# A transformer layer on one core: GpSimd's subtractions and gate products move to VectorE, and the attention output's loads become large tiles

## The chip, the cores and the metric

One core of one Trainium2 chip runs the whole layer as one program. The metric is device microseconds of one execution of that program. The engines are called PE (matrix products), DVE (VectorE), ACT (ScalarE), POOL (GpSimd) and SP (SyncE, which issues every DMA of this kernel, in order).

## What is computed

The reference, cut to the part around the change (1024 positions, 1024 features, all float32):

```python
h = h + 0.5 * swiglu(rms_norm(h, norm_ffn1), ffn1_gate, ffn1_up, ffn1_down)
u = rms_norm(h, norm_mix)
xc, bg, cg, q, k, v, g_conv, g_attn = split(u @ w_in)
y_conv = short_gated_conv(xc, bg, cg, conv_w) @ w_conv_out
q, k = apply_rope(q), apply_rope(k)              # 4 heads, two q/k sets of 64 each, v of 128
# for each block of 128 queries: p = softmax(mask(q k^T / 8)); a = p[set 0] - lam * p[set 1]
o = a @ v
o = rms_norm(o, subln_g) * (1 - lambda_init)     # per head, over its 128 features
y_attn = o @ w_attn_out
h = h + (sigmoid(g_conv) * y_conv + sigmoid(g_attn) * y_attn) @ w_o
h = h + 0.5 * swiglu(rms_norm(h, norm_ffn2), ffn2_gate, ffn2_up, ffn2_down)
return rms_norm(h, norm_final)
```

## The kernel before

Everything is kept feature-major (128 features on the partitions, 512 positions in a tile's row). A float32 product is made of three PE products of two halves: each operand is split into a rounded high part (`hi`, a copy) and what is left (`lo`, a subtraction), and hi·hi, hi·lo and lo·hi are summed in PSUM. So each operand that PE reads costs one copy, mostly on ACT (L248), and one subtraction of a 128x512 tile (L243), on DVE or on POOL: `split` (L245) has two fractions, and its share counter sends that part of the subtractions to POOL.

The program runs in stages, one after the other: the first feed-forward block (to about 640 us), the input projection of the mixer, **attention** (about 1013 to 1228 us), the **conv output**, the **heads' norm**, the **attention output**, the product with **w_o** (from 1334.5 us) and the second feed-forward block.

**Attention** (`attend`) goes over 16 units, a unit being a head and a pair of query blocks of 128. A unit has four scores (two query blocks, two sets); each is some matmuls (L955) with a mask product (L957), a row maximum on DVE (L966), an exponential on ACT (L972, L973), then a scaling on POOL (L981), the subtraction of the second set on DVE (L987 to L989), transposes on PE (L1001), their split, and the product with v (L1031). The k and q tiles are split by hand: high part on ACT (L943 for q), low part on POOL (L919 for k, 16 times, L944 for q, 16 times). Between these steps `fill()` puts pieces of six matmuls of other work on PE: first the gates of the mixer (`plain`, L1159), which is the remainder of the input projection, then blocks of the conv output. Within this part the order on PE, DVE, ACT and POOL is the order of the code (`manual_schedule`); after it a scheduler orders them. A unit uses two PSUM banks for scores ("sc"), two for transposes ("at"), one for its result ("ot"), and one ("ps") is left for the filling work.

**Conv output and attention output** are both `merge`: 16 blocks, a block being 12 matmuls of 128x512 (L1221) for 128 output features and half of the positions (t). For each block one gate tile (L1199) and, once per 128 features, one weight tile (L1192) are loaded into tiles of the pool C, which has ten. Conv blocks are evicted by an ACT copy (L1229) and a POOL multiply with the gate (L1230); attention blocks get a sigmoid on ACT (L1201), a DVE multiply (L1236) and a DVE add. The **heads' norm** (`normed`) lies between them: for each half t and head a square on ACT (L1293), a product with ones on PE (L1295), `rstd_light` (L446 to L450, three C tiles, its product on POOL) and a DVE multiply (L1300). Then `res` (L267 the matmuls, L398 the eviction) makes the product with w_o.

The piece that sets the order of the filling work before, and the eviction of a conv block:

```python
                if c == 6:
                    yield
...
                def ready(ms=ms, ps=ps, g=g):
                    nc.scalar.copy(ms, ps)
                    nc.gpsimd.tensor_tensor(ms, ms, g, ALU.mult)
```

`ready` runs at the next `settle()` of `attend`, that is right behind the next score.

Of the kernel before, what the change touches and what calls it, by code (L numbers as in the profile page):

```python
# [12 lines left out]
F32 = mybir.dt.float32  # L13
# [5 lines left out]
P = 128  # L19
# [140 lines left out]
class K:  # L160
# [281 lines left out]
    def rstd_light(self, ps, n):  # L442

        nc = self.nc
        y, v, a = self.C(), self.C(), self.C()
        nc.scalar.activation(y, ps, AF.Abs_reciprocal_sqrt, bias=self.eps, scale=1.0 / n)  # L446
        nc.vector.tensor_scalar(v, ps, 0.5 / n, 0.5 * EPS, ALU.mult, ALU.add)
        nc.scalar.activation(a, y, AF.Square)
        nc.gpsimd.tensor_tensor(v, a, v, ALU.mult)
        nc.vector.scalar_tensor_tensor(a, v, -1.5, y, ALU.add, ALU.mult)  # L450
        return a
# [309 lines left out]
class Mixer:  # L761
# [139 lines left out]
    def head(self, h):  # L901
# [6 lines left out]
        for s in range(2):  # L908
# [7 lines left out]
            for a, kd in enumerate(kds):  # L916
                ks = kst[:, s, a * TH : (a + 1) * TH]
                nc.scalar.copy(ks, kd)
                nc.gpsimd.tensor_tensor(ks[64:128], kd[64:128], ks[64:128].bitcast(F32), ALU.subtract)  # L919
# [14 lines left out]
    def load_q(self, h, qp):  # L934
# [9 lines left out]
        nc.gpsimd.tensor_tensor(qs[:, 1], qraw, qs[:, 0].bitcast(F32), ALU.subtract)  # L944
# [102 lines left out]
    def attend(self, fill, late):  # L1047
# [11 lines left out]
        for n in range(len(units) + 2):  # L1059
# [57 lines left out]
            if n >= 13:  # L1117
                next(late, None)
            last = p


    def plain(self, idxs, f):
# [3 lines left out]
        for x in ((0, 1),):  # L1126
# [3 lines left out]
            for c in range(4):  # L1130
                k.split(u[:, c], hi[:, c], lo[:, c], 0.7, 0.5, "pl")
# [4 lines left out]
        def weights(i, o):  # L1136
# [3 lines left out]
            for kk in range(2):  # L1140
                a = k.t("F", [P, 2, 4, P], F32R)
                k.split(raw[i][:, o, 4 * kk : 4 * kk + 4, :], a[:, 0], a[:, 1], 1.0, 0.5, "pw")
# [36 lines left out]
    def split_y(self, src):  # L1179
        k = self.k  # L1180
        r = k.t("Q", [P, 2, 2, TH], F32R)
        for j in range(2):
            k.split(src[:, j], r[:, 0, j], r[:, 1, j], 0.7, 0.4, "y")
        return r

    def merge(self, w, yq, wsrc, m):

        k, nc = self.k, self.k.nc

        def weights(n, j, o):  # L1190
            raw = k.t("C", [P, 4, P])
            nc.sync.dma_start(raw, wsrc[j][:, o])  # L1192
            a = k.t("FA"[n % 2] if w == 1 else "F", [P, 2, 4, P], F32R)
            k.split(raw, a[:, 0], a[:, 1], 1.0, 0.5 if w == 0 else 0.0, "ma")
            return a

        def gates(j, o, t):
            g = k.C()
            nc.sync.dma_start(g, self.gd[w][j][:, 2 * o + t, :])  # L1199
            if w == 1:  # L1200
                nc.scalar.activation(g, g, AF.Sigmoid, bias=self.gate_bias(w, j, o))  # L1201
            return g

        todo = [(j, o) for j in range(4) for o in range(2)]
        if w == 0:
            seq = [(x, t) for n in range(0, 8, 2) for t in range(2) for x in todo[n : n + 2]]
        else:
            seq = [(x, t) for t in (1, 0) for x in todo]
        ws = {x: weights(n, *x) for n, x in enumerate(todo[:2])}
        for n, ((j, o), t) in enumerate(seq):  # L1210
            g = gates(j, o, t)
            a = ws[j, o]
            self.settle()
            ps = k.psd() if self.dense else k.ps()
            c = 0
            for kk in range(4):
                if c == 6:
                    yield
                b = yq[kk // 2][t]
                for x, y in ((0, 0), (0, 1), (1, 0)):  # L1220
                    nc.tensor.matmul(ps, a[:, x, kk], b[:, y, kk % 2], start=c == 0, stop=c == 11)  # L1221
                    c += 1
            if len(ws) < 8 and (w == 1 or n % 4 > 1):
                ws[todo[len(ws)]] = weights(len(ws), *todo[len(ws)])
            ms = m[o][t][:, j]
            if w == 0:

                def ready(ms=ms, ps=ps, g=g):
                    nc.scalar.copy(ms, ps)  # L1229
                    nc.gpsimd.tensor_tensor(ms, ms, g, ALU.mult)  # L1230

                self.ready = ready
                if self.dense:
                    self.settle()
            else:
                nc.vector.tensor_tensor(g, ps, g, ALU.mult)  # L1236
                k.tt(ms, ms, g, ALU.add)
            yield
# [4 lines left out]
    def run(self, raws, f, load_h, done, pre):  # L1243
# [18 lines left out]
        with k.tc.manual_schedule(engines={ET.PE, ET.DVE, ET.Activation, ET.Pool}):  # L1262
# [3 lines left out]
            def values():  # L1266

                for t in range(2):
                    for a in range(2):
# [5 lines left out]
                        for j in range(2):  # L1275
                            k.split(y[j], yq[a][t][:, 0, j], yq[a][t][:, 1, j], 1.0, 1.0, "y")
# [3 lines left out]
            def normed():  # L1280

                Y = {}
                for t in (1, 0):
                    Y[t] = k.t("Q", [P, 4, TH])
                    for a in range(2):
                        nc.sync.dma_start(Y[t][:, 2 * a : 2 * a + 2], self.od[a][t])
                for t in (1, 0):
                    pss = []
                    for a in range(2):
                        oq[a][t] = k.t("Q", [P, 2, 2, TH], F32R)  # L1290
                    for i in range(4):
                        sq = k.C()
                        nc.scalar.activation(sq, Y[t][:, i], AF.Square)  # L1293
                        pss.append(k.psd())
                        nc.tensor.matmul(pss[i], k.ones, sq, start=True, stop=True)  # L1295
                        yield
                    for i in range(4):
                        y = Y[t][:, i]
                        r = k.rstd_light(pss[i], P)
                        nc.vector.scalar_tensor_tensor(y, y, self.gsub, r, ALU.mult, ALU.mult)  # L1300
# [155 lines left out]
```

## Time and profile before

| | |
|---|---|
| median of 3 runs | 2081.24 us (2080.03 to 2082.38) |
| the profiled execution | 2082.11 us |
| span of its profile | 2080.3 us |
| PE busy | 1981.0 us (95%) |
| DVE busy | 1402.0 us (67%) |
| ACT busy | 935.1 us (45%) |
| POOL busy | 136.8 us (7%) |
| mean granted PE clock | 0.978 of full speed |

A profile row names a line of the kernel, an engine, an operation and the tiles that it writes and reads; "[1.74 <-ACT Q L973]" behind a row says that the engine stood idle for 1.74 us before it, and which instruction's end released it. A granted clock of 1 is 2.4 GHz, 0.5 is 1.2 GHz.

### The profile page before, as it was taken

The numbers are of one execution on the slowest core, as the hardware profiler recorded it, in microseconds if no ns is written. First come the engines' busy times: TensorE is split into PE (matmuls) and PEld (weight loads), VectorE is DVE, ScalarE is ACT, GpSimd is POOL, SyncE is SP. The second block draws the span as 40 slices with busy tenths as digits, with TensorE's granted clock in tenths as the row PEclk, the third lists the DMA queues.
The fourth block names the chain that finished last, engine by engine and source line by source line (L and its number), as shares of the span: only waits on it lengthen the run. The fifth ranks groups of instructions, "written<-read, shape, count | busy, mean of one in ns | idle before, by whom it ended". The sixth has DMA issues, their size and how long they took to land.

```text
span 2080.3 us, 24145 instructions
## 1 busy us (share of the span) xinstructions
PE 1981.0 (95%) x8808; PEld 1624.7 (78%) x8808; DVE 1402.0 (67%) x2166; ACT 935.1 (45%) x1684; POOL 136.8 (7%) x123
## 2 busy tenths in 40 slices
PE   9799999999999999999799997999999999999997
PEld 8588888888877877777578775877788888888885
DVE  8965665676866856656376737798865665666874
ACT  7433333353464633233366656456433333353362
POOL 0000000000000000000244445000000000000000
PEclk9899999999999999999899998999999999999998
DMA  5223223264543423312333344423223223274441
GB/s 213 84 109 113 95 102 117 81 236 159 194 157 111 152 98 100 126 57 71 119 105 122 97 148 144 190 81 132 97 102 121 86 101 112 82 264 152 150 154 59
DMA packets 81208, 259.70 MB, mean 125 GB/s; under 512 B 10048, under 2 KB 16320, under 8 KB 63936
## 3 DMA queue, kind: packets, MB, share of 16 engines
q1 hardware_dynamic: 81088, 258.15, 34.8%
q8 instruction: 69, 1.13, 0.2%
q14 instruction: 51, 0.42, 0.1%
HBM read 183.14 MB, written 74.97 MB: 124 GB/s over the span
## 4 chain that ended last, share of the span: by engine, by line
PE 81%; DVE 10%; ACT 3%; issue 2%; POOL 1%; DMA 1%; SPq 0%; DVEq 0%; ACTq 0%; POOLq 0%
PE sc L267 37%; PE at L267 16%; PE ps L267 9%; PE ot L267 8%; DVE Q L243 3%; PE ps L1159 2%; DVE A L243 1%; DVE C L243 1%; DVE F L243 1%; PE ps L1221 1%; PE sc L955 1%; PE sc L339 1%; PE sc L338 1%; PE sc L337 1%; PE sc L1221 1%
## 5 line engine op out<-in xcount | busy, mean ns | idle before, releaser
L267 PE MATMUL sc<-Q,A 128*128 128x512 f32 x1968 | 473.5, 390 | 2.4 <-ACT C L308 2.4
L267 PEld LDWEIGHTS sc<-Q,A 128*128 128x128 f32 x1968 | 369.7, 188 | 81.3 <-ACT C L308 3.2
L267 PE MATMUL sc<-Q,F 128*128 128x512 f32 x1548 | 382.1, 396 | 29.5 <-ACT Q L248 11.4
L267 PEld LDWEIGHTS sc<-Q,F 128*128 128x128 f32 x1548 | 294.6, 191 | 96.9 <-ACT Q L248 12.9
L243 DVE TENSOR_TENSOR F<-Q,F 128x512 fp32r<-128x512 f32 (+1 forms) x307 | 211.8, 696 | 170.1 <-ACT F L248 169.7
L248 ACT CAST F<-Q 128x512 fp32r<-128x512 f32 (+1 forms) x315 | 190.0, 612 | 256.5 <-PE sc L267 88.1
L243 DVE TENSOR_TENSOR Q<-Q,Q 128x512 fp32r<-128x512 f32 (+4 forms) x334 | 278.7, 887 | 33.6 <-ACT Q L248 26.8
L248 ACT CAST A<-Q 128x512 fp32r<-128x512 f32 (+1 forms) x299 | 180.3, 611 | 268.0 <-PE sc L267 159.1
L243 DVE TENSOR_TENSOR A<-Q,A 128x512 fp32r<-128x512 f32 (+1 forms) x299 | 202.0, 678 | 130.2 <-ACT A L248 129.3
L267 PE MATMUL at<-Q,F 128*128 128x512 f32 x1128 | 279.4, 393 | 10.1 <-ACT C L308 9.2
L267 PEld LDWEIGHTS at<-Q,F 128*128 128x128 f32 x1128 | 213.0, 189 | 57.3 <-ACT C L308 10.9
L248 ACT CAST Q<-Q 128x512 fp32r<-128x512 f32 (+1 forms) x214 | 153.1, 759 | 87.0 <-DVE Q L243 31.1
L243 DVE TENSOR_TENSOR C<-C,C 128x512 f32<-128x512 f32 x236 | 161.5, 688 | 16.6 <-DMA C<-zd 5.0
L243 DVE TENSOR_TENSOR Q<-Q 128x512 f32<-128x512 f32 x216 | 148.3, 690 | 3.7
L267 PE MATMUL ps<-Q,A 128*128 128x512 f32 x498 | 124.2, 390 | 0.0
L308 ACT COPY C<-sc 128x512 f32<-128x512 f32 x88 | 51.4, 588 | 156.5 <-PE sc L267 155.4
L267 PE MATMUL ot<-Q,A 128*128 128x512 f32 x450 | 112.8, 392 | 0.9 <-DVE Q L398 0.9
L267 PEld LDWEIGHTS ps<-Q,A 128*128 128x128 f32 x498 | 93.6, 188 | 19.6 <-issue 0.3
L1159 PE MATMUL ps<-Q,F 128*128 128x512 f32 x384 | 105.9, 412 | 3.1 <-ACT C L1165 3.1
L267 PE MATMUL at<-Q,A 128*128 128x512 f32 x444 | 107.6, 389 | 0.8 <-DVE C L310 0.8
L310 DVE TENSOR_TENSOR C<-C,sc 128x512 f32<-128x512 f32 x81 | 55.6, 687 | 75.3 <-ACT C L308 35.1
L267 PEld LDWEIGHTS ot<-Q,A 128*128 128x128 f32 x450 | 85.3, 190 | 19.0 <-issue 1.3
(218 smaller groups left out, 2190.6 us busy)
## 6 DMA issues: line engine op xcount, KB each, us to landing
Q<-in_ffn_gate SPq DMA_DIRECT2D x21, 1024.0 KB, 5.8
Q<-in_ffn_up SPq DMA_DIRECT2D x21, 1024.0 KB, 4.8
Q<-in_w_in SPq DMA_DIRECT2D x20, 1024.0 KB, 5.4
g1d<-C SPq DMA_DIRECT2D x77, 256.0 KB, 2.0
g2d<-C SPq DMA_DIRECT2D x77, 256.0 KB, 2.0
Q<-in_ffn_down SPq DMA_DIRECT2D x16, 1024.0 KB, 6.5
Q<-g1d SPq DMA_DIRECT2D x14, 1024.0 KB, 6.3
Q<-g2d SPq DMA_DIRECT2D x14, 1024.0 KB, 5.8
```

The costliest lines, as they stand in the source:

```text
L243: e.tensor_tensor(out, a, b, op)
L248: self.nc.scalar.copy(hi, src)
L267: mm = lambda *x, **kw: self.nc.tensor.matmul(*x, skip_group_check=True, **kw)
L308: nc.scalar.copy(C[o, t], ps)
L310: nc.vector.tensor_tensor(C[o, t], C[o, t], ps, ALU.add)
L337: mm(ps, a[:, 0, q], hi[:, q], start=n == q == 0, stop=False)
L338: mm(ps, a[:, 0, q], lo[:, q], start=False, stop=False)
L339: mm(ps, a[:, 1, q], hi[:, q], start=False, stop=n == 1 and q == 3)
L955: nc.tensor.matmul(sc[:, a : a + w], qs[:, hl, s, qb * P : (qb + 1) * P], kst[:, s, a : a + w], start=hl == 0, stop=hl == 1 and a + w < n)
L1159: nc.tensor.matmul(ps, a[kk][:, x, q], y[:, q], start=c == 0, stop=c == 23)
L1221: nc.tensor.matmul(ps, a[:, x, kk], b[:, y, kk % 2], start=c == 0, stop=c == 11)
```

## The change

- `rstd_light`: the product that POOL made is made by DVE, and the tile of the squares is passed in and used again, so that a head takes two further C tiles, not three.
- The low parts of k and q (L919, L944), and of every `split` in attention, conv output and norm, are made by DVE. POOL keeps the softmax scaling (L981), 32 instructions.
- `merge` is replaced by `conv_out` and `attn_out`. A conv block's weights and gate are loaded one block ahead; its 12 matmuls are one piece, where they were two of six; the eviction is one DVE instruction that multiplies the PSUM bank with the gate. Both halves t of a weight tile come one after the other.
- `attn_loads` loads the weights of the attention output, ahead of the norm of half 0, into two Q tiles of 1 MB by four DMAs; the gates come as four Q tiles of 1 MB.
- `normed(t)` is made once per half. Half 1 (`self.tail`) starts in the last two rounds of `attend`, with two steps in each, and its PSUM tiles are there those of the scores.

```diff
@@ rstd_light @@
-    def rstd_light(self, ps, n):
+    def rstd_light(self, ps, n, a):
 
         nc = self.nc
-        y, v, a = self.C(), self.C(), self.C()
+        y, v = self.C(), self.C()
         nc.scalar.activation(y, ps, AF.Abs_reciprocal_sqrt, bias=self.eps, scale=1.0 / n)
         nc.vector.tensor_scalar(v, ps, 0.5 / n, 0.5 * EPS, ALU.mult, ALU.add)
         nc.scalar.activation(a, y, AF.Square)
-        nc.gpsimd.tensor_tensor(v, a, v, ALU.mult)
+        nc.vector.tensor_tensor(v, a, v, ALU.mult)
         nc.vector.scalar_tensor_tensor(a, v, -1.5, y, ALU.add, ALU.mult)
         return a
@@ head (k) and load_q (q) @@
-                nc.gpsimd.tensor_tensor(ks[64:128], kd[64:128], ks[64:128].bitcast(F32), ALU.subtract)
+                nc.vector.tensor_tensor(ks[64:128], kd[64:128], ks[64:128].bitcast(F32), ALU.subtract)
-        nc.gpsimd.tensor_tensor(qs[:, 1], qraw, qs[:, 0].bitcast(F32), ALU.subtract)
+        nc.vector.tensor_tensor(qs[:, 1], qraw, qs[:, 0].bitcast(F32), ALU.subtract)
@@ attend, end of each round @@
+            if n >= 16:
+                for _ in range(2):
+                    next(self.tail, None)
+                    fill()
@@ plain @@
-                k.split(u[:, c], hi[:, c], lo[:, c], 0.7, 0.5, "pl")
+                k.split(u[:, c], hi[:, c], lo[:, c], key="pl")
-                k.split(raw[i][:, o, 4 * kk : 4 * kk + 4, :], a[:, 0], a[:, 1], 1.0, 0.5, "pw")
+                k.split(raw[i][:, o, 4 * kk : 4 * kk + 4, :], a[:, 0], a[:, 1], key="pw")
@@ merge goes; conv_out, block, attn_loads, attn_out come @@
+    def conv_out(self, yq, m):
+        k, nc = self.k, self.k.nc
         todo = [(j, o) for j in range(4) for o in range(2)]
+        ws, gs = {}, {}
+        def load(n):
+            if n < 16:
+                (j, o), t = seq[n]
+                if t == 0:
+                    raw = k.t("C", [P, 4, P])
+                    nc.sync.dma_start(raw, k.io["w_conv_out"][j][:, o])
+                    a = ws[j, o] = k.t("F", [P, 2, 4, P], F32R)
+                    k.split(raw, a[:, 0], a[:, 1], key="ma")
+                g = gs[n] = k.C()
+                nc.sync.dma_start(g, self.gd[0][j][:, 2 * o + t, :])
+        seq = [(x, t) for x in todo for t in range(2)]
+        load(0)
         for n, ((j, o), t) in enumerate(seq):
+            load(n + 1)
+            a, g = ws[j, o], gs.pop(n)
             self.settle()
             ps = k.psd() if self.dense else k.ps()
+            self.block(ps, a, yq, t)
+            if not self.dense:
+                yield
+            def ready(ms=m[o][t][:, j], ps=ps, g=g):
+                nc.vector.tensor_tensor(ms, ps, g, ALU.mult)
+            self.ready = ready
+            if self.dense:
+                self.settle()
+            yield
+    def block(self, ps, a, yq, t):
+        c = 0
+        for kk in range(4):
+            b = yq[kk // 2][t]
+            for x, y in ((0, 0), (0, 1), (1, 0)):
+                self.k.nc.tensor.matmul(ps, a[:, x, kk], b[:, y, kk % 2], start=c == 0, stop=c == 11)
+                c += 1
+    def attn_loads(self):
+        k, nc = self.k, self.k.nc
+        self.wa = []
+        for i in range(2):
+            w = k.t("Q", [P, 2, 2, 4, P])
+            for x in range(2):
+                nc.sync.dma_start(w[:, x], k.io["w_attn_out"][2 * i + x])
+            self.wa.append(w)
+    def attn_out(self, oq, m):
+        k, nc = self.k, self.k.nc
+        todo = [(j, o) for j in range(4) for o in range(2)]
+        ws, gs = {}, {}
+        def weights(n):
+            j, o = todo[n]
+            a = ws[j, o] = k.t("FA"[n % 2], [P, 2, 4, P], F32R)
+            k.split(self.wa[j // 2][:, j % 2, o], a[:, 0], a[:, 1], key="ma")
+        def gates(j):
+            g = gs[j] = k.t("Q", [P, 4, TH])
+            nc.sync.dma_start(g, self.gd[1][j])
+        def sigmoid(j, o, t):
+            g = gs[j][:, 2 * o + t]
+            nc.scalar.activation(g, g, AF.Sigmoid, bias=self.gate_bias(1, j, o))
+        for j in range(2):
+            gates(j)
+        for n in range(2):
+            weights(n)
+        for t in (1, 0):
+            for n, (j, o) in enumerate(todo):
+                if t == 1 and n in (2, 4):
+                    gates(n // 2 + 1)
+                sigmoid(j, o, t)
+                ps = k.psd()
+                self.block(ps, ws[j, o], oq, t)
+                if t == 1 and n + 2 < 8:
+                    weights(n + 2)
+                g, ms = gs[j][:, 2 * o + t], m[o][t][:, j]
                 nc.vector.tensor_tensor(g, ps, g, ALU.mult)
                 k.tt(ms, ms, g, ALU.add)
-            yield
@@ in the attention block @@
-                            k.split(y[j], yq[a][t][:, 0, j], yq[a][t][:, 1, j], 1.0, 1.0, "y")
+                            k.split(y[j], yq[a][t][:, 0, j], yq[a][t][:, 1, j], key="y")
-            def normed():
...
+            def normed(t):
+                Y = k.t("Q", [P, 4, TH])
+                for a in range(2):
+                    nc.sync.dma_start(Y[:, 2 * a : 2 * a + 2], self.od[a][t])
+                    oq[a][t] = k.t("Q", [P, 2, 2, TH], F32R)
+                yield
+                todo = []
+                def square(i):
+                    sq = k.C()
+                    nc.scalar.activation(sq, Y[:, i], AF.Square)
+                    ps = k.psd() if self.dense else k.ps("sc")[:, :TH]
+                    nc.tensor.matmul(ps, k.ones, sq, start=True, stop=True)
+                    todo.append((sq, ps))
+                square(0)
+                yield
+                for i in range(4):
+                    if i < 3:
+                        square(i + 1)
+                    sq, ps = todo.pop(0)
+                    y = Y[:, i]
+                    r = k.rstd_light(ps, P, sq)
+                    nc.vector.scalar_tensor_tensor(y, y, self.gsub, r, ALU.mult, ALU.mult)
+                    k.split(y, oq[i // 2][t][:, 0, i % 2], oq[i // 2][t][:, 1, i % 2], key="oq")
+                    yield
             def filling():
                 yield from self.plain(range(ns, NWP), f)
                 for _ in late:
                     pass
-                yield from self.merge(0, yq, io["w_conv_out"], m)
+                yield from self.conv_out(yq, m)
 
             late = values()
+            self.tail = normed(1)
             fill = filling()
             next(fill)
             self.attend(lambda: next(fill, None), late)
             self.settle()
         self.dense = True
         k.rot, k.halves = 0, deque()
-        for _ in normed():
+        for _ in self.tail:
             next(fill, None)
+        self.attn_loads()
+        for _ in normed(0):
             next(fill, None)
         for _ in fill:
             pass
-        for _ in self.merge(1, oq, io["w_attn_out"], m):
-            pass
+        self.attn_out(oq, m)
```

Three places of the instruction order.

DVE, attention, unit of head 0 and the largest query pair (`sm` holds maxima and sums, `sc` the scores, `A` tiles are operands of PE). Before:

```order
L966 TENSOR_REDUCE sm_7683<-sc_7671 128x1
L243 TENSOR_TENSOR A_7685<-at_7677,A_7685 128x512
L966 TENSOR_REDUCE sm_7683<-sc_7705 128x1
L243 TENSOR_TENSOR A_7716<-at_7711,A_7716 128x256
L243 TENSOR_TENSOR A_7716<-at_7711,A_7716 128x128
L987 RECIPROCAL sm_7626<-sm_7626 128x1
```

Now:

```order
L966 TENSOR_REDUCE sm_7683<-sc_7671 128x1
L243 TENSOR_TENSOR A_7685<-at_7677,A_7685 128x512
L944 TENSOR_TENSOR A_7611<-C_7608,A_7611 128x512
L966 TENSOR_REDUCE sm_7683<-sc_7705 128x1
L243 TENSOR_TENSOR A_7716<-at_7711,A_7716 128x256
L243 TENSOR_TENSOR A_7716<-at_7711,A_7716 128x128
L987 RECIPROCAL sm_7626<-sm_7626 128x1
```

The low part of the next unit's q stands ahead of the maximum of the fourth score.

PE, the last round of attention, blocks 2 to 5 of the conv output (`ps` their bank). Before:

```order
L1221 MATMUL ps_9365<-Q_8972,F_9287 128x512 x6
L955 MATMUL sc_9372<-Q_8429,A_9152 128x256 x2
L957 MATMUL sc_9372<-msk_3248 128x64
L1221 MATMUL ps_9365<-Q_9037,F_9287 128x512 x6
L1221 MATMUL ps_9397<-Q_9135,F_9282 128x512 x6
L1031 MATMUL ot_9356<-A_9349,Q_8430 128x256 x3
```

Now:

```order
L955 MATMUL sc_9379<-Q_8429,A_9152 128x256 x2
L957 MATMUL sc_9379<-msk_3248 128x64
L1224 MATMUL ps_9397<-Q_8972,F_9361 128x512 x6
L1224 MATMUL ps_9397<-Q_9037,F_9361 128x512 x6
L1031 MATMUL ot_9352<-A_9345,Q_8430 128x256 x3
```

A block starts right behind a score, where half a block stood there before. On DVE the evictions (L1212) of those blocks stand now:

```order
L966 TENSOR_REDUCE sm_9343<-sc_9379 128x1
L987 RECIPROCAL sm_9303<-sm_9303 128x1
L988 TENSOR_TENSOR sm_9303<-sm_9303,nlam_3258 128x1
L989 SCALAR_TENSOR_TENSOR Q_9302<-Q_9302,sm_9303 128x128
L980 RECIPROCAL sm_9343<-sm_9343 128x1
L1212 TENSOR_TENSOR Q_7192<-ps_9366,C_9287 128x512
L987 RECIPROCAL sm_9343<-sm_9343 128x1
```

The eviction is the sixth instruction from the score's maximum on; before, it was an ACT copy and a POOL multiply.

SP, the DMAs around the start of the attention output (`gd` gates, `od` the heads' results). Before:

```order
L1199 DMA C_9749<-gd_3230 128x512
L1192 DMA C_9818<-in_w_attn_out 128x512
L1192 DMA C_9823<-in_w_attn_out 128x512
L1199 DMA C_9828<-gd_3231 128x512
L1192 DMA C_9844<-in_w_attn_out 128x512
```

Now:

```order
L1234 DMA Q_9633<-in_w_attn_out 128x1024 x2
L1234 DMA Q_9636<-in_w_attn_out 128x1024 x2
L1317 DMA Q_9639<-od_3223 128x1024
L1317 DMA Q_9639<-od_3225 128x1024
L1194 DMA C_9663<-in_w_conv_out 128x512
```

The weights are asked for ahead of the last loads of the conv output and of the norm's half 0, and not behind them.

## Rows read from the trace of the kernel before

**Rows 1.** The page: the span, and the busy time of each engine.

```profile
span 2080.3 us, 24145 instructions
...
PE 1981.0 (95%) x8808; PEld 1624.7 (78%) x8808; DVE 1402.0 (67%) x2166; ACT 935.1 (45%) x1684; POOL 136.8 (7%) x123
```

**Rows 2.** Busy time by stretch: length, PE, PEld, DVE, ACT, POOL, clock, DMA share, GB/s.

```profile
1032.00:1212.00 180.00, 170.27 (x971) 144.64 (x970) 119.20 (x237) 118.67 (x309) 82.18 (x70) 0.99 0.33 106
...
1276.00:1296.00 20.00, 10.26 (x27) 6.28 (x26) 17.75 (x21) 10.80 (x17) 7.06 (x5) 0.66 0.49 155
...
1334.00:1385.00 51.00, 45.62 (x189) 35.86 (x188) 51.00 (x79) 24.24 (x44) 0.00 (x0) 0.97 0.16 63
```

**Rows 3.** Waits, 1000 to 1232 us: engine, line, releaser: total, times, longest.

```profile
PE sc L955 <- ACT Q L973: 4.0, 3, 1.7
PE sc L955 <- POOL A L944: 3.4, 6, 1.1
```

**Rows 4.** Groups of POOL, 940 to 1290 us: busy, mean ns, idle before and releaser.

```profile
L944 POOL TENSOR_TENSOR A<-C,A 128x512 fp32r<-128x512 f32 x16 | 20.7, 1295 | 30.5 <-ACT A L943 24.9 <-PE sc L957 4.1 <-ACT sm L972 1.3
...
L981 POOL TENSOR_SCALAR Q<-Q,sm 128x1024 f32<-128x1024 f32 x4 | 4.6, 1139 | 7.9 <-DVE sm L980 4.5 <-DVE sm L987 3.3
```

**Rows 5.** Groups of DVE, 1005 to 1232 us.

```profile
L243 DVE TENSOR_TENSOR A<-at,A 128x512 fp32r<-128x512 f32 x24 | 16.5, 689 | 17.3 <-ACT A L248 16.7
L243 DVE TENSOR_TENSOR F<-Q,F 128x512 fp32r<-128x512 f32 x7 | 10.4, 1481 | 0.8 <-ACT F L248 0.8
```

**Rows 6.** Timeline of a large unit: start, duration, instruction, idle time before.

```profile
1070.87 1.23 DVE L966 TENSOR_REDUCE sm<-sc 128x1 f32<-128x1024 f32 x1 [0.37 <-PE sc L957]
...
1071.28 0.61 ACT L943 CAST A<-C 128x512 fp32r<-128x512 f32 x1
```

**Rows 7.** Timeline of PE at the two changes from a large unit to the next.

```profile
1081.59 1.20 PE L955 MATMUL sc<-Q,A 128*128 128x512 f32 x4 [1.74 <-ACT Q L973]
...
1178.59 1.20 PE L955 MATMUL sc<-Q,A 128*128 128x512 f32 x4 [1.74 <-ACT Q L973]
```

**Rows 8.** Timeline of the last round, 1226 to 1232 us.

```profile
1226.01 0.42 DVE L966 TENSOR_REDUCE sm<-sc 128x1 f32<-128x256 f32 x1 [0.90 <-PE sc L957]
...
1227.07 0.15 DVE L980 RECIPROCAL sm<-sm 128x1 f32<-128x1 f32 x1
...
1228.11 1.65 PE L1221 MATMUL ps<-Q,F 128*128 128x512 f32 x6 [0.68 <-ACT Q L1229]
...
1230.24 0.52 PE L1001 MATMUL at<-ident,Q 128*128 128x128 f32 x3
...
1231.96 0.29 DVE L243 TENSOR_TENSOR A<-at,A 128x128 fp32r<-128x128 f32 x1 [0.33 <-ACT A L248]
```

**Rows 9.** Timeline of PE, end of the conv output to the attention output.

```profile
1268.50 1.12 PE L1295 MATMUL sc<-C,ones 128*128 128x512 f32 x2 [0.43 <-ACT Q L1229]
...
1286.42 1.22 PE L1221 MATMUL sc<-Q,F 128*128 128x512 f32 x2 [8.66 <-ACT F L248]
1287.66 1.22 PE L1221 MATMUL ps<-Q,A 128*128 128x512 f32 x2
1289.94 4.39 PE L1221 MATMUL sc<-Q,F 128*128 128x512 f32 x10 [1.05 <-DVE F L243]
1294.17 2.45 PE L1221 MATMUL ps<-Q,A 128*128 128x512 f32 x10
```

**Rows 10.** Waits of SP's queue, 1255 to 1300 us.

```profile
SPq L1199 <- DVE C L450: 15.2, 4, 4.7
SPq L1192 <- DVE C L450: 13.7, 1, 13.7
```

**Rows 11.** Timeline of PE and DVE in the product with w_o.

```profile
1334.53 0.39 PE L267 MATMUL ps<-Q,A 128*128 128x512 f32 x1
...
1340.34 0.50 PE L267 MATMUL sc<-Q,F 128*128 128x512 f32 x1 [0.20 <-ACT Q L248]
...
1352.51 0.69 DVE L398 SCALAR_TENSOR_TENSOR Q<-at,Q 128x512 f32<-128x512 f32 x1
...
1375.82 4.60 PE L267 MATMUL sc<-Q,F 128*128 128x512 f32 x12 [2.75 <-DVE Q L398]
...
1382.10 2.88 PE L267 MATMUL sc<-Q,F 128*128 128x512 f32 x12
```

More of the change, by code (lines that the diff above doesn't have):

```diff
@@ L1176, in plain @@
         self.settle()
[L1179 to L1186, printed above, removed]
-        k, nc = self.k, self.k.nc
[L1190 to L1202, printed above, removed]
-        todo = [(j, o) for j in range(4) for o in range(2)]
[L1205 to L1209, printed above, removed]
+    def conv_out(self, yq, m):
+        k, nc = self.k, self.k.nc
+        todo = [(j, o) for j in range(4) for o in range(2)]
+        ws, gs = {}, {}
[11 more added lines that the diff above has]
+        load(0)
@@ L1210, in merge @@
         for n, ((j, o), t) in enumerate(seq):
-            g = gates(j, o, t)
-            a = ws[j, o]
+            load(n + 1)
+            a, g = ws[j, o], gs.pop(n)
             self.settle()
             ps = k.psd() if self.dense else k.ps()
-            c = 0
-            for kk in range(4):
-                if c == 6:
-                    yield
[L1219 to L1235, printed above, removed]
+            self.block(ps, a, yq, t)
+            if not self.dense:
+                yield
@@ L1236, in merge @@
                 nc.vector.tensor_tensor(g, ps, g, ALU.mult)
                 k.tt(ms, ms, g, ALU.add)
-            yield
     NPLAIN = 4
@@ L1275, in values @@
                         for j in range(2):
-                            k.split(y[j], yq[a][t][:, 0, j], yq[a][t][:, 1, j], 1.0, 1.0, "y")
+                            k.split(y[j], yq[a][t][:, 0, j], yq[a][t][:, 1, j], key="y")
             oq = [[None, None], [None, None]]
-            def normed():
[L1282 to L1300, printed above, removed]
-                        k.split(y, oq[i // 2][t][:, 0, i % 2], oq[i // 2][t][:, 1, i % 2], 1.0, 0.0, "oq")
-                        yield
```

## The prediction

> **What bounds the kernel now.** I read the page first: PE is busy 1981.0 of 2080.3 us [rows 1], so the time follows PE, and an edit is worth what it does to PE's idle time. The whole loss is about 99 us over the program, and the change touches only the stretch from about 1013 to 1385 us. The table by stretch shows there where PE stands still [rows 2]: 9.7 us of the 180 in attention, 9.7 of 20 around 1286, 5.4 of 51 in the product with w_o. The clock stands beside it: 0.99, 0.66, 0.97. The waits and the timelines tell what each was for. In attention PE waits for POOL's low part of q 3.4 us in all, and 4.0 us for an exponential [rows 3]. Around 1286 it waits 8.66 us for a weight tile's high part [rows 9]; behind it SP held that load 13.7 us until a C tile came free [rows 10]. In the product with w_o it waits for DVE's evictions, and DVE is busy for all 51.00 us [rows 2, 11]. So the three places have three limits: the softmax chain, a C tile, DVE.
>
> **Attention.** Removed: the 3.4 us of waits on POOL [rows 3], six of them. A low part takes 1295 ns on POOL [rows 4] and should take 689 on DVE, as any subtraction of that size does undisturbed [rows 5].
>
> Added: DVE is in order, and the q subtraction stands ahead of the fourth score's maximum (first place of the order). In a large unit that maximum starts at 1070.87, while ACT's cast of q runs from 1071.28 for 0.61 [rows 6]. The subtraction can't start before 1071.89 and ends at 1071.89 + 0.69 = 1072.58, so the maximum is 1.7 us later. The exponential, the transposes' splits and the next subtraction follow on the same two engines; I add 0.4 for one DVE instruction that now falls the wrong way, 2.1 us in all. Where PE waits for that exponential today, this adds to PE's wait: at the changes between two large units, twice, 1.74 us each [rows 7], so 2 × 2.1 = 4.2 us. Elsewhere PE doesn't wait for it, and the filling matmuls cover it. The sum is 4.2 − 3.4 = **+0.8 us**. Bounds: −3.4 if the delay is covered everywhere, +8 if it falls on four units and no wait goes.
>
> DVE's load grows by 16 (k) + 16 (q) + 8 (plain weights) + 8 (conv values) = 48 subtractions × 0.689 = 33 us. Some returns: seven weight subtractions on DVE take 1481 ns each instead of 689 [rows 5], and POOL makes the other half of these at the same time; without that, 7 × 0.79 = 5.5 us come back. In attention DVE goes from 119.2 of 180 us, 66% [rows 2], to about 80%. I price this at nothing, because PE's filling work stands between scores; if that cover is gone, the third rival below is what happens.
>
> A rule speaks against this part. The rows: of equal subtractions those beside POOL's take twice as long [rows 5]. The Trainium skill, "SBUF — State Buffer", section "SBUF: two separate sides", says that a DVE instruction with two SBUF inputs and a GpSimd instruction that reads SBUF exclude each other for the whole of the first one. By that rule the moved subtractions, which all have two SBUF inputs, would hold back the scaling that stays on POOL by up to one subtraction, and at the two large changes this would make the sum about 2 × 0.7 = 1.4 us longer than by the rows alone. By the rows the scaling of a large unit takes 1139 ns [rows 4] and nothing on PE waits for it; I keep +0.8.
>
> **The plain gates' end to the first conv block.** The high and low parts of weights and values are made in the same place, by DVE alone instead of two engines. One doubled instruction gets shorter, others come ahead of it: 0.
>
> **Conv output, norm, attention output (1216 to 1334).** Removed, all on PE:
> - four short waits on evictions, weights and norm tiles, the first 0.68 [rows 8], the last 0.43 [rows 9]: 2.1 us together. The eviction is one DVE instruction, the weights come a block earlier.
> - the wait for the weights of the attention output: 8.66 + 1.05 = 9.7 us [rows 9]. The four loads now stand ahead of the norm of half 0 on SP and go to Q tiles, so the C tile that held SP for 13.7 us [rows 10] is no longer in the way. And half 1 is normalised before the conv output ends, so PE has attention blocks to do while half 0 is not.
> - the slow clock behind that wait: 14 matmuls take 1.22 + 1.22 + 4.39 = 6.8 us, where ten take 2.45 at full clock [rows 9], so 3.4 us are lost.
>
> Together −15.2 us. Added:
> - Block 3 of the conv output now starts right behind a score, from the single bank "ps", so it waits for the eviction of block 2, which stands sixth on DVE (second place). From the maximum's start to the end of the fifth instruction are 1227.07 + 0.15 − 1226.01 = 1.2 us [rows 8]; the eviction adds 0.69, a subtraction of a PSUM bank being the nearest row [rows 5], and 0.2 for the hand-over: 2.1 us.
> - Block 4 waits for an eviction behind the transposes' splits: from 1230.24 to 1231.96 + 0.29 = 2.0 us [rows 8], + 0.69 − 0.4 that PE has other work: 2.3 us.
> - Later, at four places, an eviction, a weight tile, a C tile or the reading of the heads' results (behind 2 MB of weights on SP's queue) may be late. No row of before shows these; from below they are 0, from above the 2.3 of block 4. I take one DVE instruction and a hand-over, 0.69 + 0.4 = 1.1, nearer to the rows of DVE in this stage: 4.4 us.
> - A fall of the clock behind one of these waits: a wait of 2.75 was followed by twelve matmuls in 4.60 instead of 2.88 [rows 11], 1.7 lost; waits of 1.74 were not [rows 7]. Half of it: 0.9.
>
> Together +9.7, the sum **−5.5 us**. Bounds −13 (nothing is added but block 3) and +2 (every place costs its upper bound, the clock falls twice).
>
> **Product with w_o (1334 to 1385).** Nothing in it is edited; what is late is DVE. It enters the stage with evictions and gate additions of the attention output left over, its first eviction of w_o comes at 1352.51, 18 us after the first matmul at 1334.53 [rows 11], and PE waits five times from 0.20 to 2.75 us, 5.4 together [rows 11], three of them, 4.5 us, for evictions. The gates' loads were held 15.2 us by C tiles [rows 10]; as large tiles they are there early, so evictions keep step with the blocks. Two or three blocks of two instructions of 0.69 less in arrears are 3 to 4 us; I take 3. Then of 4.5 us of waits 1.5 stay, less than the 1.74 that left the clock alone, and of the 1.7 us at a slow clock 1.5 come back: **−4.5 us**. Bounds 0 (DVE is no less late) and −7.1 (all goes).
>
> **The sum.** 0.8 − 5.5 − 4.5 = −9.2; 2082.1 − 9.2 = 2072.9 us. The profiled execution took 2082.11 us, 0.9 over the median of the runs and inside their spread (2080.03 to 2082.38), so I give 2073.
>
> **The rivals.**
> 1. *All waits after attention go, and attention stays as it is.* For it: conv weights and gates are loaded a block ahead, and POOL is gone from every chain there. Against it: block 3's wait follows from the order itself. Time: −13 − 7 + 0, about 2062.
> 2. *The hole is filled by another wait.* The weights of the attention output stand behind conv gates on SP that wait for C tiles, or the norm of half 1, which needs score banks and DVE, ends too late; then PE waits some 8 us for DVE instead of for a weight, at a low clock behind it. For it: DVE is busy 17.75 of 20 us around the hole [rows 2] and gets eight more products and all low parts. Time: +0.8 in attention, little elsewhere, about 2081.
> 3. *Slower: the softmax chain turns DVE-bound.* A q or weight subtraction ahead of a maximum delays that unit by 2.1 us, not only at the two places where PE waits today. The gains are 5.5 + 4.5 + 3.4 = 13.4 us, so it decides from 13.4 / 2.1, six to seven of the 16 units on. With ten units it is 21 − 13.4 = +7.6, about 2090. For it: DVE at 80%, every one of its instructions in the chain of one unit's exponentials, and POOL's own wait for ACT's cast, which now becomes DVE's (24.9 us over the units [rows 4]). Against it: PE waits for an exponential only three times today [rows 3].
>
> **How the numbers follow.** Forecast (2067 to 2078) 0.40, first rival 0.20, second 0.20, third 0.20. A measurement of this kernel can tell 0.2%, 4.2 us: faster is under 2077.1, slower over 2085.4. The forecast gives 0.38 faster and 0.02 the same, the first rival 0.20 faster; the second 0.03 faster, 0.15 the same, 0.02 slower; the third 0.03 the same, 0.17 slower. So 0.61, 0.20 and 0.19. The range reaches from the first rival, 2061, to 2088, which leaves out half of the third and the end of the first.
>
> **What would show it.** Right: POOL keeps 32 scalings and nothing else in attention; no score waits for POOL; the waits for an exponential grow from 1.7 to near 4 us at the two large changes; two conv blocks wait about 2 us each for the eviction at L1212; no wait over 3 us between 1230 and 1334 and a clock near 1; in the product with w_o fewer waits for L398. Wrong: a long PE wait around the attention output on DVE or on a load (second rival), waits for L973 or L944 in most units (third), or waits for L398 as before, which would take the term of −4.5 away.

## The result: slower by 0.74%, and all of it in attention

| | before | changed |
|---|---|---|
| median | 2080.95 us (4 runs, 2080.03 to 2082.38) | 2096.61 us (4 runs, 2093.0 to 2099.31) |
| ratio | | 1.0074, 95% interval 1.0056 to 1.0091 |

The forecast was 2073 us, in a range from 2061 to 2088. The time lies outside it and on the other side.

The page of the changed kernel, to be set beside [rows 1]:

```profile
span 2097.5 us, 24054 instructions
...
PE 1987.3 (95%) x8808; PEld 1629.1 (78%) x8808; DVE 1427.2 (68%) x2242; ACT 927.5 (44%) x1670; POOL 25.5 (1%) x45
```

POOL's subtractions and products are gone, as the change says; the scaling stays. DVE's busy time grew by 25 us only, over the whole program of 2080 us, so DVE's load alone need not be the whole story.

The table by stretch, set beside [rows 2]: attention up to the first conv block, the start of the attention output, the first 47 us of the product with w_o.

```profile
1032.00:1234.00 202.00, 177.81 (x974) 149.37 (x972) 136.08 (x276) 118.40 (x310) 22.39 (x29) 0.97 0.31 97
1268.00:1300.00 32.00, 27.40 (x101) 18.84 (x101) 23.45 (x37) 18.35 (x31) 0.00 (x0) 0.95 0.52 182
1353.00:1400.00 47.00, 43.38 (x183) 35.15 (x182) 47.00 (x73) 23.28 (x42) 0.00 (x0) 0.96 0.18 65
```

The first stretch holds the same 970-odd matmuls as before, in 202 us instead of 180. PE stands still 24.2 us of it, before 9.7: that is 14.5 of the 22 us. The other 7.5 us are in the matmuls themselves, busy 177.8 us instead of 170.3 at a granted clock of 0.97 instead of 0.99. DVE is busy 136.1 of 202, that is 67%, before 66%: it did not become the busy engine that the third rival needed at 80%. The last maximum of attention starts at 1249.71 instead of 1226.01, 23.7 us later. From there to the first matmul of w_o (1353.87, before 1334.53) it takes 104.2 us instead of 108.5. From that matmul to a point further on that is the same in both kernels (2561 matmuls start from there to the end, in each) it takes 144.6 us instead of 146.3. The point, before and then changed:

```profile
1480.82 2.88 PE L267 MATMUL ot<-Q,F 128*128 128x512 f32 x12
```

```profile
1498.48 2.88 PE L267 MATMUL ot<-Q,F 128*128 128x512 f32 x12
```

So the loss is in attention, and what comes behind it gave back about 6 us.

PE's waits in attention (total, times, longest). Before, 1000 to 1232 us:

```profile
PE at L929 <- DMA C<-vd: 8.5, 1, 8.5
...
PE ps L1159 <- ACT C L1165: 3.1, 8, 0.7
```

Changed, 1000 to 1234 us:

```profile
PE ps L1163 <- ACT C L1169: 16.4, 14, 1.8
PE at L929 <- DMA C<-vd: 8.9, 1, 8.9
PE sc L955 <- ACT Q L973: 4.7, 5, 1.9
PE sc L955 <- ACT A L943: 2.3, 4, 1.2
PE sc L955 <- DVE A L944: 1.2, 5, 0.3
```

Before, PE waited 3.1 us for the copy on ACT that empties the bank of the filling matmuls (L1165 there, L1169 now). Now it is 16.4 us, in 14 waits. What I took for cover, the filling matmuls, is itself what waits. The long wait for a load (L929) is as long as before.

What DVE waits for tells why. Before, and then changed, 1024 to 1226 us:

```profile
DVE sm L966 <- PE sc L957: 29.9, 31, 2.9
DVE A L243 <- ACT A L248: 25.2, 37, 2.5
```

```profile
DVE A L944 <- ACT A L943: 19.0, 14, 1.8
DVE A L243 <- ACT A L248: 18.3, 26, 1.4
...
DVE sm L966 <- PE sc L957: 7.8, 6, 2.5
DVE Q L989 <- POOL Q L981: 6.1, 8, 1.1
DVE Q L919 <- ACT Q L918: 4.8, 6, 1.0
```

Before, DVE waited 29.9 us for scores: it was ahead of PE. Now it waits 19.0 us for ACT's cast of q, standing before a maximum whose score is already there, and only 7.8 us for scores. So DVE's waits for scores, which were its slack, have largely become waits for fresh casts. Its work in the stretch grew as well, from 119.2 to 136.1 us; which of the two costs PE the time, the experiments have to tell.

One unit in the timeline, before and then changed, the same fourth score:

```profile
1057.95 0.61 ACT L943 CAST A<-C 128x512 fp32r<-128x512 f32 x1
1058.15 0.96 DVE L966 TENSOR_REDUCE sm<-sc 128x1 f32<-128x768 f32 x1 [0.89 <-PE sc L957]
...
1059.14 0.20 ACT L972 ACTIVATE sm<-sm 128x1 f32<-128x1 f32 x1 [0.58 <-DVE sm L966]
...
1060.27 0.57 ACT L1165 COPY C<-ps 128x512 f32<-128x512 f32 x1
```

```profile
1061.96 0.60 ACT L943 CAST A<-C 128x512 fp32r<-128x512 f32 x1
1062.59 0.69 DVE L944 TENSOR_TENSOR A<-C,A 128x512 fp32r<-128x512 f32 x1 [1.34 <-ACT A L943]
...
1063.20 0.95 DVE L966 TENSOR_REDUCE sm<-sc 128x1 f32<-128x768 f32 x1
...
1064.19 0.20 ACT L972 ACTIVATE sm<-sm 128x1 f32<-128x1 f32 x1 [1.63 <-DVE sm L966]
...
1065.32 0.58 ACT L1169 COPY C<-ps 128x512 f32<-128x512 f32 x1
...
1065.94 2.77 PE L1163 MATMUL ps<-Q,F 128*128 128x512 f32 x6 [1.72 <-ACT C L1169]
```

From the cast to the maximum: 0.20 us before, 1.24 now. ACT then stands for 1.63 us instead of 0.58, and the copy that frees the filling bank, which is behind the exponential on ACT, comes 3.4 us after the cast instead of 2.3. PE waits 1.72 us for it, where it had no wait at that place before, and the six matmuls behind the wait take 2.77 us at a granted clock of 0.54, where six behind a wait of 0.68 took 1.65 [rows 8].

### The profile page after: what moved, and what is told of

The parts are those of the page before. It is cut to its first block, busy times and chain, and to the rows that moved or that the text cites. A ratio compares the mean times of both kernels' runs of the same rounds, so it can differ in the third digit from the quotient of the medians.

```text
span 2097.5 us, 24054 instructions
## 1 busy us (share of the span) xinstructions
PE 1987.3 (95%) x8808; PEld 1629.1 (78%) x8808; DVE 1427.2 (68%) x2242; ACT 927.5 (44%) x1670; POOL 25.5 (1%) x45
## 4 chain that ended last, share of the span: by engine, by line
PE 80%; DVE 11%; ACT 4%; issue 3%; DMA 1%; POOL 0%; SPq 0%; DVEq 0%; ACTq 0%; POOLq 0%
PE sc L267 36%; PE at L267 16%; PE ps L267 9%; PE ot L267 8%; DVE Q L243 3%; PE ps L1163 1%; DVE sm L966 1%; PE ps L1224 1%; PE sc L1224 1%; DVE A L243 1%; PE at L1224 1%; DVE C L243 1%; PE sc L339 1%; PE sc L338 1%; PE sc L337 1%
## 5 line engine op out<-in xcount | busy, mean ns | idle before, releaser
L243 DVE TENSOR_TENSOR Q<-Q,Q 128x512 fp32r<-128x512 f32 (+4 forms) x352 | 287.6, 867 | 32.5 <-ACT Q L248 25.6
L1163 PE MATMUL ps<-Q,F 128*128 128x512 f32 x384 | 109.3, 423 | 16.4 <-ACT C L1169 16.4
L267 PEld LDWEIGHTS ps<-Q,A 128*128 128x128 f32 x498 | 93.6, 188 | 19.3
```

The costliest lines, as they stand in the source:

```text
L243: e.tensor_tensor(out, a, b, op)
L267: mm = lambda *x, **kw: self.nc.tensor.matmul(*x, skip_group_check=True, **kw)
L1163: nc.tensor.matmul(ps, a[kk][:, x, q], y[:, q], start=c == 0, stop=c == 23)
```

## Experiments

Two theories. **Theory Q**: DVE waits in order for a fresh cast, and the chain maximum, exponential, copy waits behind it. **Theory L**: DVE has too many subtractions in attention.

**Give back one at a time.** The edits on the changed kernel, the first in `q_pool`, the second in `k_pool`, both in `qk_pool`:

```diff
-        nc.vector.tensor_tensor(qs[:, 1], qraw, qs[:, 0].bitcast(F32), ALU.subtract)
+        nc.gpsimd.tensor_tensor(qs[:, 1], qraw, qs[:, 0].bitcast(F32), ALU.subtract)
...
-                nc.vector.tensor_tensor(ks[64:128], kd[64:128], ks[64:128].bitcast(F32), ALU.subtract)
+                nc.gpsimd.tensor_tensor(ks[64:128], kd[64:128], ks[64:128].bitcast(F32), ALU.subtract)
```

> The changed kernel with only q's low part (L944) back on POOL. Theory Q (in DVE's in-order queue that one subtraction waits for ACT's cast of q, and the fourth score's maximum, its exponential and the copy that frees PE's filling bank wait behind it): PE's waits for L1169 fall from 16.4 us to under 7, the last maximum of attention comes 12 to 20 us earlier than 1249.7, and the run takes 2077 to 2085 us. Theory L (DVE simply has too much to do in attention, 48 subtractions more): a third of the load goes, so a third of the 23.7 us of delay comes back, 8 us: 2087 to 2091.

> The changed kernel with only k's low part (L919) back on POOL, also 16 subtractions. Theory Q: k's subtractions don't stand behind a fresh cast ahead of a maximum in most units, so little comes back, 0 to 4 us: 2092 to 2098. Theory L: as much as for q, 8 us: 2087 to 2091.

> The changed kernel with the low parts of both q and k back on POOL; the weights' and values' low parts stay on DVE. From the two runs that gave back one each (12.6 and 5.0 us): if the two act apart, 2096.6 - 17.6 = 2079; if they share DVE's slack (q's wait only hurts because k used the slack up), the second gives less than alone, 2080 to 2084.

Measured: `q_pool` 2083.99 us (ratio to the kernel before 1.0014, 1.0003 to 1.0024), `k_pool` 2091.63 (1.0053, 1.0036 to 1.007), `qk_pool` 2080.36 (0.9997, 0.9988 to 1.0007). So q is worth 12.6 us, k 5.0, both 16.2: the whole loss sits in these 32 subtractions. Sixteen of q cost more than twice as much as sixteen of k, against theory L; but k costs more than theory Q had given it, and `k_pool` falls between the two ranges. In `q_pool` the wait for L1169 is 2.8 us, and the last maximum comes 19.3 us earlier, both as theory Q had it.

**One at a time on the kernel before.** The same two edits the other way, POOL to DVE:

> The kernel before with only q's low part (L944) moved to DVE. Theory Q: most of the delay of the whole change comes with this one edit, 10 to 18 us: 2091 to 2099. Theory L: a third of it or less, since DVE gets 16 subtractions of 48, 0 to 8 us: 2081 to 2089.

> The kernel before with only k's low part (L919) on DVE. If DVE in the kernel before has idle time enough for work that waits for nothing fresh: 2080 to 2083, and the 5 us that k cost in the changed kernel come from its slack being gone. If each subtraction ahead of a maximum costs by itself: 2084 to 2088.

Measured: `b_q_dve` 2089.47 us (1.0045, 1.0027 to 1.0062), `b_k_dve` 2089.5 (1.0034, 1.0021 to 1.0047). By the medians each costs about 8 us. For q that is less than theory Q had said and just over the range of theory L. The rows show the chain all the same. DVE's waits in `b_q_dve`, 1005 to 1226 us, then PE's, 1000 to 1234 us:

```profile
DVE A L944 <- ACT A L943: 19.5, 15, 2.1
...
DVE sm L966 <- PE sc L957: 10.1, 13, 2.4
```

```profile
PE ps L1159 <- ACT C L1165: 13.5, 14, 1.7
```

With q's subtractions alone DVE waits 19.5 us for their casts, and PE waits 13.5 us for the copy that empties the filling bank, before 3.1. For k both theories had missed it. DVE's waits in `b_k_dve`, 1005 to 1226 us:

```profile
DVE sm L966 <- PE sc L957: 21.7, 20, 3.1
DVE A L243 <- ACT A L248: 21.0, 32, 1.4
DVE Q L919 <- ACT Q L918: 8.4, 10, 1.9
```

k's subtraction also follows its own cast (L918), and DVE waits 8.4 us for it, ten times. PE pays for it elsewhere: in `b_k_dve` the low part of q, still on POOL, holds PE 6.4 us instead of 3.4 [rows 3]. So theory Q may hold for k too. This is not shown: no run hides k's wait, and the 11 us of work of its 16 subtractions on DVE are a rival that stays.

**The same instructions, the wait hidden.** Here q's low part stays on DVE and moves one step, behind the fourth score's maximum; the cast stays. On the changed kernel it is `q_late`, on the kernel before `b_q_late`; `q_late_k_pool` is `q_late` with k on POOL.

```diff
         nc.scalar.copy(qs[:, 0], qraw)
+        yield
         nc.vector.tensor_tensor(qs[:, 1], qraw, qs[:, 0].bitcast(F32), ALU.subtract)
...
             on(self.peak, u, 1, 1)
+            next(ql, None)
```

> The changed kernel with q's low part still on DVE, but one step later, behind the fourth score's maximum, while the cast on ACT stays where it is. DVE makes the same instructions. Theory Q: the wait for the cast is hidden behind the maximum, 12 to 20 us come back: 2077 to 2085. Theory L: nothing changes, 2093 to 2099.

> The kernel before with q's low part on DVE, behind the fourth score's maximum (the run b_q_dve had it ahead of it and took 2089.5). If only the wait for ACT's cast costs, and 11 us more of DVE's time are covered by its idle time: 2080 to 2083. If DVE's added time costs as well, as in the changed kernel (2090.6 against 2084.0 with q on POOL): 2085 to 2088.

> The changed kernel with q's low part on DVE behind the fourth score's maximum and k's on POOL. If the gains add (6.0 of the later subtraction, 5.0 of k): 2085 to 2087. If both only give DVE the same slack: 2088 to 2091. If the wait for the cast was all there was to q, it comes near the run with both on POOL: 2080 to 2083.

Measured: `q_late` 2090.6 us (1.0046, 1.0031 to 1.006), `b_q_late` 2084.64 (1.0012, 1.0003 to 1.0021), `q_late_k_pool` 2085.04 (1.0012, 1.0001 to 1.0022). On the kernel before, hiding the wait takes 5 of the 8 us away; the subtractions in their later place still cost some 0.12%, and the time lies between the two cases that were written down. DVE's waits in `b_q_late`, 1024 to 1226 us (all lines below the edit are moved by one or two):

```profile
DVE sm L967 <- PE sc L958: 28.0, 30, 2.4
DVE A L243 <- ACT A L248: 25.1, 36, 2.5
...
DVE A L945 <- ACT A L943: 0.7, 2, 0.5
```

The wait for the cast is 0.7 us, and DVE waits 28.0 us for scores again, with the same instructions to make: its slack is back. PE's wait for the filling bank is 6.0 us instead of 13.5. The move takes two things out from ahead of the fourth maximum, the wait and the subtraction's own 0.69 us, and no run parts them; by the rows the wait is the larger, 19.5 us against 16 × 0.69 = 11 us.

In the changed kernel the move gives 6.0 us of q's 12.6, and with k on POOL as well 11.6 of 16.2, as the case in which the gains add had it. `q_late` lies between the ranges of the two theories. DVE still waits 4.1 us for the cast of q there, seven times, and PE 5.7 us for the filling bank. That the time of the subtractions counts too, once other waits have taken DVE's slack, would explain the rest; it is not shown.

**A step further forward.** In `q_mid` cast and subtraction of q come half a unit earlier (cast behind the second exponential, subtraction behind the third maximum).

> The changed kernel, all low parts on DVE, with the cast of q on ACT half a unit earlier (behind the second score's exponential) and its low part on DVE behind the third score's maximum. If what stayed in the run with the later subtraction (2090.6) was the wait for q itself (PE waits for L943 and for the low part), it goes: 2084 to 2088. If it is DVE's load by k, weights and values: 2089 to 2092 again. If the load of q lands too late for a cast there, ACT waits for it in the small units and the time is over 2093.

Measured: 2091.98 us (1.0057, 1.0041 to 1.0074). The middle case, and no better than `q_late`: waiting for q is gone on DVE (0.4 us), but ACT now waits 5.4 us for q's load, DVE 13.6 us for k's cast (4.8 in the changed kernel), and PE 4.7 us for the split of a transposed tile and 9.3 us for exponentials (4.7 in the changed kernel). A step taken forward lands on somebody else's wait.

**The rest of the change alone.** `att_pool` is `qk_pool` with the weights' and values' low parts on POOL in their old shares as well.

> The changed kernel with every low part of the attention stage on POOL as before (q, k, half of the plain weights, the conv values): what is left of the change is the conv output, the heads' norm and the attention output. By the prediction's terms for those, -5.5 and -4.5: 2071 to 2073. If their gain is what the trace of the changed kernel shows between the last maximum and the first matmul of w_o (108.5 to 104.1 us) and behind it, 4 to 6 us: 2075 to 2077. If it is nothing: 2081.

Measured: 2078.74 us (0.999, 0.9976 to 1.0004): between the last two cases, a gain of some 2 us that can't be told from none, where the forecast's two terms for these stages gave −10. PE's timeline shows what took the hole's place [rows 9]:

```profile
1229.89 4.21 PE L1224 MATMUL ps<-Q,F 128*128 128x512 f32 x12 [1.99 <-DVE sm L987]
1237.58 4.61 PE L1224 MATMUL ps<-Q,F 128*128 128x512 f32 x12 [2.14 <-DVE Q L1212]
1243.07 2.99 PE L1224 MATMUL ps<-Q,F 128*128 128x512 f32 x12 [0.87 <-DVE Q L1212]
...
1258.57 0.73 PE L1224 MATMUL at<-Q,F 128*128 128x512 f32 x2 [1.06 <-ACT F L248]
...
1277.51 1.98 PE L1326 MATMUL sc<-C,ones 128*128 128x512 f32 x4 [3.39 <-ACT C L1324]
```

The hole of 8.66 us is gone, but here are 9.5 us in five waits (three more, 0.23, 0.88 and 1.00 us, make it 11.6), and two blocks at a lower clock, 0.67 and 0.63 granted, take 4.21 and 4.61 us where the third takes 2.99 at 1.00. The first wait is for the eviction, though its row names L987: L1212 ends just before that instruction.

**Two edits on that kernel.** `halves` cuts the conv blocks into two pieces of six again while attention runs. `y0_first` loads half 0 of the heads' results ahead of the 2 MB of weights. `both` has both.

```diff
-            self.block(ps, a, yq, t)
-            if not self.dense:
-                yield
+            c = 0
+            for kk in range(4):
+                if c == 6 and not self.dense:
+                    yield
...
-        self.attn_loads()
-        for _ in normed(0):
+        norm0 = normed(0)
+        next(norm0)
+        self.attn_loads()
+        for _ in norm0:
```

> The kernel of the run att_pool (all low parts of attention on POOL, the rest of the change in), with the conv blocks cut into two pieces of six matmuls again while attention runs; the eviction stays one DVE instruction. Theory B (a block of twelve in one slot is followed by a slot without work, so its eviction comes a step later and PE waits at L1224 for the one bank 1.99, 2.14 and 0.87 us and loses 3 to 4 us to the slower clock behind it): these waits fall under 1 us each and 5 to 8 us come back, 2071 to 2074. Theory H (the waits only move, since the transposes' chain sets the pace at the end of attention): 2077 to 2080.

> The kernel of att_pool with the loads of the heads' results of half 0 issued ahead of the 2 MB of weights of the attention output. If the product with ones (L1326) waits 3.39 us because its operand queues behind those weights, this wait goes: 2075 to 2077. If PE then waits as long for something else (weights of the conv output or of the attention output), 2078 to 2081.

> Both edits together on att_pool. If the two waits are apart in time and both cost what the trace shows: 2068 to 2072, faster than the kernel before by 9 us or more. If what one gives up the other takes: 2074 to 2079.

Measured: `halves` 2076.01 us (0.9973, 0.9961 to 0.9985), `y0_first` 2079.08 (0.9986, 0.9976 to 0.9996), `both` 2077.44 (0.9978, 0.9968 to 0.9988). `halves` beats the kernel before by 0.27%. Its conv blocks, whose matmuls and eviction stand at L1213 and L1217:

```profile
1224.18 1.62 PE L1213 MATMUL ps<-Q,F 128*128 128x512 f32 x6 [1.15 <-DVE sm L987]
1228.96 3.01 PE L1213 MATMUL ps<-Q,F 128*128 128x512 f32 x12 [0.78 <-DVE Q L1217]
```

1.99 and 2.14 became 1.15 and 0.78, and the clock stayed up behind them. That is half of what was expected: 2.7 us by the medians, not 5 to 8, between the two theories. Part of it was lost again further on, where a wait for a weight tile is 2.42 us instead of 1.06 and six matmuls just behind it take 3.31 us at a granted clock of 0.54:

```profile
1249.95 0.74 PE L1213 MATMUL at<-Q,F 128*128 128x512 f32 x2 [2.42 <-ACT F L248]
...
1251.05 3.31 PE L1213 MATMUL ps<-Q,F 128*128 128x512 f32 x6
```

In `y0_first` the wait of 3.39 us is replaced by 1.47, 1.53 and 0.66 us at the same place, so nothing that can be told is gained, and `both` is not better than `halves` alone.

## Why the prediction was wrong

**Attention, forecast +0.8; its last maximum came 23.7 us later.** This is the step that failed. The order was read rightly (the subtraction ahead of the maximum, 1.7 us later), and so was the end of the 3.4 us of waits on POOL. Wrong was "elsewhere PE doesn't wait for it, and the filling matmuls cover it". The filling matmuls have one bank, and the copy that empties it stands on ACT behind the exponential that waits: 16.4 us instead of 3.1. The eight waits of 3.1 us were in the trace of before, and the prediction has no term for them. The delay was charged in two places, at the exponentials of the two large changes, 2.1 us each; there PE waits 1.90 and 1.91 us instead of 1.74 twice. It came in 14 other places. The sum for attention also has no term for the clock, which took about a third of the loss (7.5 of 22 us). And k's 16 subtractions were priced at nothing, as load of DVE, though they too stand behind a cast; they cost 5.0 us in the changed kernel and 7.8 on the kernel before. The pieces add up roughly, by medians: q 8 and k 7.8 on the kernel before, weights and values 1.6 (`qk_pool` to `att_pool`, within the spread of the runs), the rest −2, together 15.4; measured 15.7.

**The third rival** came closest, at a chance of 0.20 and with a time, 2090, that was too short. Its "DVE at 80%" was not needed: DVE is at 67% and waits. What it named in passing, that POOL's wait for the cast becomes DVE's, is what the rows of q show (19.0 us). Its sign, waits for L973 or L944 in most units, was not what came: the waits are for L1169.

**The rule on the shared SBUF port.** The weights' subtractions on DVE fell from 1481 ns [rows 5] to 687 once POOL made none beside them, and take 1481 again in `att_pool`, where POOL makes half of them. This agrees with the rule in the Trainium skill, "SBUF — State Buffer", section "SBUF: two separate sides", that a DVE instruction with two SBUF inputs and a GpSimd instruction that reads SBUF exclude each other. The charge worked out from it, a scaling on POOL held back, doesn't show in the row of the large units: 1121 ns for 1024 columns, 1139 before [rows 4]. That row doesn't test it either, since none of the four scalings runs at the same time as a moved subtraction.

```profile
L981 POOL TENSOR_SCALAR Q<-Q,sm 128x1024 f32<-128x1024 f32 x4 | 4.5, 1121 | 30.4 <-DVE sm L987 16.6 <-DVE sm L980 7.3 <-PE sc L957 6.5
```

**Conv output, norm, attention output, forecast −5.5.** The removed part was right: the hole of 8.66 + 1.05 us is gone. So were the two places of the eviction: 1.99 and 2.14 us against 2.1 and 2.3. Too low were the later waits (six, 7.4 us, in `att_pool`, against four of 1.1; the longest is the norm's behind the weights, 3.39) and the clock (two blocks lose 1.2 and 1.6 us against 0.9 in all). From the last maximum to w_o `att_pool` takes 107.8 us, the kernel before 108.5: −0.7. In the profile of the changed kernel itself it is −4.4: the wait of the norm is 1.38 us there, and the two blocks were not followed by a lower clock. So that near hit is in part luck: in eight other traces both blocks ran at the lower clock (last section).

**Product with w_o, forecast −4.5.** DVE stayed the bound: 47.00 us busy of 47. PE's waits for L398 became fewer, not shorter:

```profile
1373.32 4.58 PE L267 MATMUL at<-Q,F 128*128 128x512 f32 x12 [2.97 <-DVE Q L398]
...
1393.99 3.01 PE L267 MATMUL sc<-Q,F 128*128 128x512 f32 x12 [0.65 <-DVE Q L398]
```

3.6 us in two waits instead of 4.5 in three [rows 11], and the longest again with a lower clock behind it. The stage and what follows it, up to the block shown in the first section, gained 1.7 us in the changed kernel and 2.4 in `att_pool`. The step took DVE's lateness for two or three blocks' evictions left over and counted on 3 us less of them; DVE has no gap in the stage all the same, and what it is late with was not taken apart further.

## What to carry to other kernels

When work moves to an in-order engine, don't price it by its length and by that engine's share of busy time. Ask what the moved instruction waits for, and what stands behind it: a subtraction of 0.69 us placed right behind its own cast made the engine wait up to 1.8 us, 14 times, and moving it behind one independent instruction took 5 of 8 us back where there was slack. And cover is only cover if it doesn't hang on the same chain: here the filling matmuls needed a copy that stood behind the delayed exponential.

## What the runs showed of the hardware that was not expected

Waits of the same length were followed by a lower clock in one place and not in another. Blocks of twelve matmuls behind a wait of 1.99 and 2.14 us took 4.21 and 4.61 us in `att_pool`, at a granted clock of 0.67 and 0.63, and 2.98 and 3.02 in the changed kernel, at 1.00:

```profile
1251.66 2.98 PE L1224 MATMUL ps<-Q,F 128*128 128x512 f32 x12 [1.99 <-DVE sm L987]
...
1257.78 3.02 PE L1224 MATMUL ps<-Q,F 128*128 128x512 f32 x12 [2.14 <-DVE Q L1212]
```

The changed kernel's trace is the exception: in all eight other traces with these two blocks (`q_pool`, `k_pool`, `qk_pool`, `q_late`, `q_late_k_pool`, `q_mid`, `att_pool`, `y0_first`) both took 4.21 to 4.61 us, at 0.63 to 0.67. Each trace is one execution, so this may differ from one execution to the next: ten of `att_pool` took from 2070.57 us at a mean granted clock of 0.986 to 2082.94 at 0.979.

Within one trace it differs too. In the changed kernel a wait of 1.72 us at 1065.94 was followed by six matmuls in 2.77 us, at a granted clock of 0.54, and the same wait later by six in 1.65, at 1.00:

```profile
1173.80 1.65 PE L1163 MATMUL ps<-Q,F 128*128 128x512 f32 x6 [1.72 <-ACT C L1169]
```

So the length of the one wait ahead doesn't tell what it costs here. The forecast's 0.9 us, half a chance of one fall, was too little for the stage: the two blocks lose 2.8 us in `att_pool`. What decides was not tried.
